# Splitting the mixer's weights ahead of time, in the first FFN, and keeping them in DRAM as halves

## The chip, the cores and the metric

The kernel runs on one core of a Trainium2 chip. The metric is the device time of one execution in microseconds (us). Engines are named as in the profile: PE is the tensor engine, DVE the vector engine, ACT the scalar engine, POOL is GpSimd, and SP is the engine whose queue issues the DMAs here.

## The reference

One step of an encoder layer on 1056 rows (1024 of a prompt, 32 of a running stream) of width 1024:

```python
x = x + 0.5 * swiglu(rmsnorm(x, g_ffn1), w1g, w1u, w1d)          # first FFN, 1024 -> 2816 -> 1024
mix, k, v, s = token_mixer(rmsnorm(x, g_mix), w_in, ...)         # the mixer
x = x + mix
x = x + 0.5 * swiglu(rmsnorm(x, g_ffn2), w2g, w2u, w2d)          # second FFN
return rmsnorm(x, g_final), k, v, s
# token_mixer: h @ w_in gives q, k, v of 8 stick-breaking heads (64 wide) and q, k, v, r of 4
# heads of gated linear attention (GLA); y = concat(norm(o_sb), norm(o_gla) * silu(r)) @ w_out
```

Everything is float32. The tensor engine multiplies operands that are rounded to a shorter form (`F32R`), so the kernel writes each operand as a sum of two halves, hi and lo, and makes three products: hi*hi, hi*lo, lo*hi.

## The kernel before

**The split.** `split_to` makes the halves: ACT copies the source to hi, which rounds it, and then DVE (or, with `pool=True`, POOL) subtracts hi from the source to get lo. `mm3` makes the three products. Activations lie with the feature on the partition: `S.x[d]` (8 tiles of 128x1056, float32) and `S.h[d]` (their halves, 128x2x1056).

**The stages.** First FFN: gate and up products, then down products; the mixer; the second FFN, built as the first. In the FFNs, gate and up weights are worked off in 20 steps (`gate_up`, ten pairs of a gate step and an up step, class `Step`). Each step makes the seven products of a Strassen-Winograd scheme in the order `ORDER = (1, 6, 7, 5, 2, 4, 3)`, 24 matmuls of 264 columns each. While a step's products run, the sums and splits of the next step's weights are made (`prep`, `split_w`; POOL makes the sums). After an up step, the hidden blocks B11, B22, B21 and four differences of them (T1, T3, T2, T4) are split and stored to DRAM by `keep`, from where the down stage reads them as parts. `keep` uses four of the x tiles in turn as its buffers; `S.x[4]` to `S.x[7]` hold the blocks.

**The mixer.** Each weight slab of 128x1024 is loaded by `load_split`: a DMA into a buffer of pool `raw` (two buffers, tile `wraw`, 512 KB), and then a split into a buffer of pool `wp` (two buffers, tile `whl`). The lo half comes from POOL in 24 projections (`proj`, from `w_in`) and in the four slabs `slab_a` of `w_out`; for the last four slabs (`slabs_b`, in a pool of their own, `slb`) it comes from DVE. A projection is 3 chunks of 352 columns by 8 feature tiles by 3 products, 72 matmuls (tile `pj`); an output group is 12 matmuls (tile `po`). The work on PE is interleaved: `run(items, fill)` spreads the fillers (projections, output groups) among the items (the blocks of an attention), in proportion to their costs. There are two GLA rounds and then four rounds of stick-breaking attention, one for each pair of heads. A block of scores is two sigmoids on ACT, a running product (the scan) and a product on DVE, transposes on PE, a split by ACT and DVE, and the value product on PE.

**The gates.** The four projections of r (`gate(0)` to `gate(3)`) multiply the GLA output. Two of the outputs lie in `S.x[6]`, `S.x[7]`, and two are parked in DRAM (`os`). The last round but one (pair 2) has `gate(1)` and then `gate(3)` as its last fillers; at the start of pair 3 the four gated outputs are split into `S.h[4]` to `S.h[7]`, chunk by chunk, and `ready(k)` splits the outputs of the first three pairs into `S.h[0]` to `S.h[2]` with POOL.

**What sets the order.** The code gives the work in program order; a scheduler then places each instruction in its engine's stream by its own estimate. At run time every engine, and SP's queue of DMAs too, works strictly in its order: a DMA whose wait is not over holds up all those behind it on SP.

## Time and profile before

| | |
|---|---|
| three runs | 2151.09 us median (2148.07 to 2152.23) |
| the profiled execution | 2149.15 us, of which 2147.4 us is the span of instructions |
| granted TensorE clock, mean | 0.988 |
| PE / DVE / ACT / POOL busy | 2069.2 / 1442.3 / 892.2 / 742.8 us |
| first FFN, gate and up steps | from about 86 us to about 500 us |
| first FFN, down | to 737 us |
| mixer | 737 us to about 1400 us |
| second FFN | from there to the end |

The profile is read by stage: which engine is never idle there, and what ends the idle time of PE where PE has some. A busy PE is not a PE at its peak, since matmuls overlap; the distance between the starts of two matmuls tells the pace. `PEclk` is the clock that was granted to PE, as a share of full speed.

### The profile page before, as it was taken

The page shows a single profiled execution, that of the slowest core. Times are in us where ns is not written, and L with a number is a line of the kernel's source. Part 1 is how long each engine was busy: PE and PEld are TensorE (multiplying, and loading weights), DVE is VectorE, ACT ScalarE, POOL GpSimd, SP SyncE. Part 2 cuts the span into 40 slices and gives each one's busy share as a digit, 9 for nine tenths or more (in the row PEclk, how much of TensorE's full clock was granted, in tenths as well). Part 3 has the DMA queues.
Part 4 walks back from the last instruction along what each step waited for, and adds up shares of the span by engine and source line. Part 5 has one row for each costly group of instructions (what it writes and reads, how often), then busy time and mean ns, then how long its engine had stood idle before and what let it go on. Part 6 is the DMA issues. An engine that isn't in the chain of part 4 may idle for free.

```text
span 2147.4 us, 38446 instructions
## 1 busy us (share of the span) xinstructions
PE 2069.2 (96%) x15636; PEld 1998.0 (93%) x15636; DVE 1442.3 (67%) x2142; ACT 892.2 (42%) x1586; POOL 742.8 (35%) x609
## 2 busy tenths in 40 slices
PE   7999999999999999999999988899999999999997
PEld 6899999999999978888888987899999999999997
DVE  6856756646786766286776687687567667467865
ACT  6533433432233443335555555454334333322333
POOL 0134334345872321122223312101343343458720
PEclk9999999999999999999999999999999999999999
DMA  5134434449823200102203141231344334498322
GB/s 174 50 120 152 161 121 154 168 139 379 303 94 117 87 32 30 38 31 67 77 23 100 36 124 69 78 123 51 120 159 156 127 143 168 139 376 300 106 65 82
DMA packets 106705, 270.49 MB, mean 126 GB/s; under 512 B 10432, under 2 KB 31200, under 8 KB 106528
## 3 DMA queue, kind: packets, MB, share of 16 engines
q1 hardware_dynamic: 106528, 268.03, 35.6%
q8 instruction: 123, 2.02, 0.4%
q14 instruction: 54, 0.44, 0.1%
HBM read 174.46 MB, written 86.77 MB: 122 GB/s over the span
## 4 chain that ended last, share of the span: by engine, by line
PE 77%; DVE 13%; ACT 3%; issue 3%; DMA 2%; POOL 1%; DVEq 0%; SPq 0%; ACTq 0%; POOLq 0%
PE acc_a L335 11%; PE acc_c L335 11%; PE acc_d L335 11%; PE acc_b L335 5%; PE acc L243 4%; PE pj L60 3%; PE pj L61 3%; PE pj L62 3%; PE pd_c L516 3%; PE pd_a L516 2%; PE pd_d L516 2%; DVE f L1206 2%; PE pd L60 2%; PE pd L62 2%; PE pd L61 2%
## 5 line engine op out<-in xcount | busy, mean ns | idle before, releaser
L335 PE MATMUL acc_a<-h,whl 128*128 128x264 f32 x1920 | 250.1, 286 | 1.8 <-DVE whl L55 1.8
L335 PE MATMUL acc_d<-part,S 128*128 128x264 f32 x1920 | 246.6, 284 | 0.0
L335 PEld LDWEIGHTS acc_a<-h,whl 128*128 128x128 f32 x1920 | 241.6, 190 | 2.1 <-DVE whl L55 2.1
L335 PEld LDWEIGHTS acc_d<-part,S 128*128 128x128 f32 x1920 | 238.7, 188 | 0.0
L60 PE MATMUL pj<-h,whl 128*128 128x352 f32 x576 | 203.9, 354 | 0.0
L61 PE MATMUL pj<-h,whl 128*128 128x352 f32 x576 | 191.1, 332 | 0.0
L62 PE MATMUL pj<-h,whl 128*128 128x352 f32 x576 | 190.8, 331 | 0.0
L51 ACT ACTIVATE S<-s 128x512 fp32r<-128x512 f32 x160 | 98.7, 627 | 183.6 <-PE acc_d L335 77.0
L51 ACT ACTIVATE x<-x 128x528 fp32r<-128x528 f32 x112 | 72.4, 647 | 180.8 <-DVE x L394 84.8
L319 POOL TENSOR_TENSOR s<-wraw,s 128x512 f32<-128x512 f32 x38 | 49.1, 1292 | 278.9 <-DVE S L55 278.9
L385 POOL TENSOR_TENSOR x<-tc,x 128x528 f32<-128x528 f32 x60 | 103.6, 1727 | 120.0 <-DVE tc L384 107.4
L53 POOL TENSOR_TENSOR whl<-wraw,whl 128x1024 fp32r<-128x1024 f32 x28 | 69.4, 2480 | 169.9 <-ACT whl L51 169.8
L55 DVE TENSOR_TENSOR x<-x 128x528 fp32r<-128x528 f32 x112 | 85.3, 761 | 63.1 <-ACT x L51 60.8
L335 PE MATMUL acc_b<-h,S 128*128 128x264 f32 x960 | 125.5, 286 | 1.5 <-ACT h L51 1.1
L335 PE MATMUL acc_c<-part,S 128*128 128x264 f32 x960 | 124.3, 284 | 0.3 <-DVE hid L255 0.3
L55 DVE TENSOR_TENSOR S<-s,S 128x512 fp32r<-128x512 f32 x160 | 122.0, 763 | 3.7 <-ACT S L51 2.5
L335 PE MATMUL acc_c<-h,A 128*128 128x264 f32 x960 | 124.2, 285 | 0.0
L335 PEld LDWEIGHTS acc_b<-h,S 128*128 128x128 f32 x960 | 121.2, 189 | 1.9 <-ACT h L51 1.3
L534 POOL TENSOR_TENSOR x<-x,u 128x528 f32<-128x528 f32 x64 | 103.5, 1624 | 49.5 <-DVE x L505 49.0
L335 PEld LDWEIGHTS acc_c<-part,S 128*128 128x128 f32 x960 | 120.0, 188 | 0.6 <-DVE hid L255 0.6
L335 PEld LDWEIGHTS acc_c<-h,A 128*128 128x128 f32 x960 | 120.4, 188 | 0.0
L306 POOL TENSOR_TENSOR s<-wraw 128x512 f32<-128x512 f32 x38 | 48.9, 1288 | 195.6 <-DVE S L55 195.6
(344 smaller groups left out, 5122.4 us busy)
## 6 DMA issues: line engine op xcount, KB each, us to landing
part_spill<-x SPq DMA_DIRECT2D x112, 528.0 KB, 2.8
h<-part_spill SPq DMA_DIRECT2D x64, 528.0 KB, 8.9
part<-part_spill SPq DMA_DIRECT2D x48, 528.0 KB, 9.6
wraw<-win SPq DMA_DIRECT2D x24, 512.0 KB, 3.4
wraw<-w1g SPq DMA_DIRECT2D x22, 512.0 KB, 3.7
wraw<-w1u SPq DMA_DIRECT2D x22, 512.0 KB, 3.4
wraw<-w1d SPq DMA_DIRECT2D x22, 512.0 KB, 3.8
wraw<-w2g SPq DMA_DIRECT2D x22, 512.0 KB, 3.5
```

The costliest lines, as they stand in the source:

```text
L51: nc.scalar.activation(hi, src, AF.Copy)
L53: nc.gpsimd.tensor_sub(lo, src, hi.bitcast(F32))
L55: nc.vector.tensor_sub(lo, src, hi.bitcast(F32))
L60: nc.tensor.matmul(out, w[:, 0, wsl], a[:, 0, asl], start=first, stop=False)
L61: nc.tensor.matmul(out, w[:, 0, wsl], a[:, 1, asl], start=False, stop=False)
L62: nc.tensor.matmul(out, w[:, 1, wsl], a[:, 0, asl], start=False, stop=last)
L243: nc.tensor.matmul(out, self.w[i](k, a), quarter(S, k, b, j), start=k == 0 and n == 0, stop=k == KT - 1 and n == 2)
L319: eng.tensor_sub(src, a12, self.s2)
L335: nc.tensor.matmul(t[:, s, :SW], w[:, a, ks], m(k, b, s), start=fresh and k == 0 and n == 0, stop=k == 3 and n == 2, skip_group_check=not ...
L385: nc.gpsimd.tensor_mul(two(hid), t, sg)
L516: nc.tensor.matmul(t[:, s, :SW], w[:, u, k * P : k * P + P], b[:, v, ss(s)], start=fresh and k == 0 and i == 0, stop=k == 1 and i == 2, sk ...
L534: nc.gpsimd.tensor_add(x[r][h], x[r][h], u)
```

## The change

`Splits` makes the halves of all mixer weights during the gate and up steps of the first FFN: in 64 chores, four in each of the first 16 steps (after products 1, 7, 2 and 3), it loads half a slab (256 KB) into `S.x[2]` or `S.x[3]`, splits it there (ACT and DVE), and stores both halves (512 KB) to a DRAM tensor of its own (`win2`, `wo2`). In the mixer, `load_halves` reads a whole slab of halves (1 MB) by one DMA, right into the buffer that PE reads; the pool `raw` is not used there. Since two x tiles are now taken, `keep` has two buffers in turn and not four, in both FFNs, and the differences T1, T3, T2, T4 are made and kept one by one after the first four products of the following gate step (`forms`), and not together at the end of the up step.

The last two gates run in turns, chunk by chunk (`g1[c] + g3[c]`), each followed by the split of that chunk's gated outputs (`gated(c)`), so that no splits are left for the start of pair 3. `ready(k)` becomes nine splits by chunk, on ACT and DVE.

```diff
-def load_split(S, src, hi_pool, tag, pool=False):
-    raw = S.raw.tile([P, 1024], F32, name="wraw", tag="wraw")
-    nc.sync.dma_start(raw, src)
-    w = hi_pool.tile([P, 2, 1024], F32R, name="whl", tag=tag)
-    split_to(S, w[:, 0], w[:, 1], raw, pool)
+def load_halves(S, src, pool, tag):
+    w = pool.tile([P, 2, 1024], F32R, name="whl", tag=tag)
+    S.nc.sync.dma_start(w.bitcast(F32), src)
     return w
+class Splits:
+    def load(self):
+        src, _, h = self.todo[self.n]
+        b = self.raw[self.n] = self.bufs[self.n % len(self.bufs)][:, :1024]
+        self.S.nc.sync.dma_start(b[:, 512:], src[:, h * 512 : h * 512 + 512])
+        self.n += 1
+    def split(self, n):
+        _, out, h = self.todo[n]
+        b = self.raw.pop(n)
+        t = b.bitcast(F32R).rearrange("p (a n) -> p a n", a=2)
+        split_to(self.S, t[:, 0], t[:, 1], b[:, 512:])
+        nc.sync.dma_start(out[:, :, h * 512 : h * 512 + 512], b.rearrange("p (a n) -> p a n", a=2))
+    def some(self):
+        if self.n == 0:
+            self.load()
+        if self.raw:
+            n = self.n - 1
+            if self.n < len(self.todo):
+                self.load()
+            self.split(n)
...
-        t = S.x[S.n_kept % 4].bitcast(F32R).rearrange("p (a n) -> p a n", a=2)
+        t = S.x[S.n_kept % 2].bitcast(F32R).rearrange("p (a n) -> p a n", a=2)
...
             steps[t].after(p)
+            if steps[t].gate is None and t:
+                steps[t - 1].forms(ORDER.index(p))
+            if t < N - 1 and p in (1, 7, 2, 3):
+                chore()
...
-                hold["w"] = load_split(S, src, S.wp, "w", True)
+                hold["w"] = load_halves(S, src, S.wp, "w")
...
-                fills = [gate(2), gate(0), gate(1) + gate(3)]
+                g1, g3 = gate(1), gate(3)
+                fills = [flat(gate(2)), flat(gate(0)), flat([g1[c] + g3[c] + [(0, lambda c=c: gated(c))] for c in range(NCH)])]
...
-                        def ready(k):
-                            split_to(S, S.h[k][:, 0], S.h[k][:, 1], S.x[k], True)
-                            nc.sync.dma_start(S.x[k], xs[k])
+                        def ready(k, c):
+                            split_to(S, S.h[k][:, 0, cs(c)], S.h[k][:, 1, cs(c)], S.x[k][:, cs(c)])
+                            if c == NCH - 1:
+                                nc.sync.dma_start(S.x[k], xs[k])
...
-                    slabs_b = [load_split(S, A["wo"][4 + j], slb, "slb") for j in range(4)]
+                    slabs_b = [load_halves(S, A["wo2"][4 + j], slb, "slb") for j in range(4)]
```

PE's order in both FFNs stays as it was; in the mixer it shifts in places. Three places matter for what follows. In the rows a name is out<-in, and a number after a name tells buffers apart.

First, DVE in the first FFN, around the turn from an up step to the next gate step. `x_76` is the whole of the eight x tiles; 128x528 subtractions of it by L55 are `keep`'s splits, those of L394 make T1 to T4, and L351 and L354 read the products 6 and 7 of the gate step. Before:

```order
L55 TENSOR_TENSOR S4_2701<-s3_2699,S4_2701 128x512
L394 TENSOR_TENSOR x_76<-x_76 128x528 x2
L55 TENSOR_TENSOR x_76<-x_76 128x528
L394 TENSOR_TENSOR x_76<-x_76 128x528
L55 TENSOR_TENSOR x_76<-x_76 128x528
L394 TENSOR_TENSOR x_76<-x_76 128x528
L55 TENSOR_TENSOR x_76<-x_76 128x528 x2
L351 TENSOR_TENSOR u2_2760<-s1_2733,acc_b_2735 128x528
```

Now (L428 makes T1 to T4, L85 is the split, and its 128x512 rows on `x_76` are the chores):

```order
L85 TENSOR_TENSOR S4_2324<-s3_2322,S4_2324 128x512
L428 TENSOR_TENSOR x_76<-x_76 128x528 x2
L85 TENSOR_TENSOR x_76<-x_76 128x528
L428 TENSOR_TENSOR x_76<-x_76 128x528 x2
L85 TENSOR_TENSOR x_76<-x_76 128x528
L381 TENSOR_TENSOR u2_2391<-s1_2356,acc_b_2366 128x528
L85 TENSOR_TENSOR S2_2401<-s2_2399,S2_2401 128x512
L85 TENSOR_TENSOR x_76<-x_76 128x512
L384 TENSOR_TENSOR u3_2429<-u2_2391,acc_c_2404 128x528
L85 TENSOR_TENSOR S3_2441<-s3_2439,S3_2441 128x512
L85 TENSOR_TENSOR x_76<-x_76 128x528
```

Two of the four keeps moved behind the reads of products 6 and 7, and chores stand between them.

Second, DVE at the end of pair 2. `h6`, `h7`, `h4`, `h5` are the gated outputs' halves, `rs`/`x` the gating, `ks` an operand of pair 3. Before, all twelve splits of gated outputs stand after the last scan of pair 2, eight of them behind `ks`:

```order
L1137 TENSOR_TENSOR ks_13389<-kf_12656,ks_13389 64x1056
L55 TENSOR_TENSOR wt_13250<-tr_13339,wt_13250 128x4x128
L55 TENSOR_TENSOR h6_90<-x_76,h6_90 128x352
L55 TENSOR_TENSOR h4_88<-h4_88 128x352
L55 TENSOR_TENSOR h5_89<-h5_89 128x352
L55 TENSOR_TENSOR h4_88<-h4_88 128x352
L55 TENSOR_TENSOR h5_89<-h5_89 128x352
L1178 TENSOR_TENSOR x_76<-avt_13375,av_13358 64x256
```

Now:

```order
L85 TENSOR_TENSOR wt_13440<-tr_13526,wt_13440 128x4x128
L85 TENSOR_TENSOR h0_84<-x_76,h0_84 128x352
L85 TENSOR_TENSOR h1_85<-x_76,h1_85 128x352
L85 TENSOR_TENSOR wt_13441<-tr_13543,wt_13441 128x4x128
L1175 TENSOR_TENSOR ks_13603<-kf_12849,ks_13603 64x1056
L85 TENSOR_TENSOR h6_90<-x_76,h6_90 128x352
L1216 TENSOR_TENSOR x_76<-avt_13579,av_13562 64x256
```

Only the last chunk's four are left there; the splits of `h0` and `h1` that POOL made now stand on DVE.

Third, SP at the end of the mixer: the loads of the output slabs. Before, the last two of `slab_a`, then `slabs_b` (from `wraw_14425` on), the reload of x tile 3, and the second FFN's first weights:

```order
L42 DMA wraw_14199<-wo 128x1024
L42 DMA wraw_14425<-wo 128x1024
L42 DMA wraw_14430<-wo 128x1024
L42 DMA wraw_14435<-wo 128x1024
L1581 DMA x_76<-x_spill 128x1056
L42 DMA wraw_14440<-wo 128x1024
L220 DMA wraw_14747<-w2g 128x1024
```

Now:

```order
L41 DMA whl_14303<-wo_split 128x2048
L41 DMA whl_14386<-wo_split 128x2048
L317 DMA wraw_15643<-w2g 128x1024
L41 DMA whl_14609<-wo_split 128x2048
L1623 DMA x_76<-x_spill 128x1056
L41 DMA whl_14611<-wo_split 128x2048
L41 DMA whl_14613<-wo_split 128x2048
L41 DMA whl_14615<-wo_split 128x2048
```

`slabs_b` are now the last four rows but for the reload of x tile 3 (L1623), which stands ahead of three of them, where it was ahead of one; and a weight load of the second FFN (`wraw_15643`), which takes a buffer that the second FFN's first slab leaves when it is split, stands ahead of all four.

More of the change, by code (lines that the diff above doesn't have):

```diff
@@ L826, in put @@
         return cb
-    return [proj(S, A["win"][16 + 2 * hp + h], put(h)) for h in range(2)]
+    return [proj(S, A["win2"][16 + 2 * hp + h], put(h)) for h in range(2)]
 def gla_items(S, A, G, hp, vs):
@@ L1450, in between @@
                     emit(parts(H))
[L1452 removed]
+            gate_up(S, H, op, steps, among, between, down.head, A["x"], Splits(S, A, (S.x[2], S.x[3])).some)
             nc.vector.tensor_copy(S.identb, consts[:, 0])
```

59 lines of the change are left out of this document (33 added, 26 removed).

## The prediction

> **What bounds the kernel now.** I read the chain of waits and the windows by stage first, then the waits inside the mixer, then its time line. The chain of waits by engine and by line first, then windows; their columns are length, busy time of PE, weight loads, DVE, ACT and POOL, granted clock, DMA share, GB/s:
>
> ```profile
> PE 77%; DVE 13%; ACT 3%; issue 3%; DMA 2%; POOL 1%; DVEq 0%; SPq 0%; ACTq 0%; POOLq 0%
> PE acc_a L335 11%; PE acc_c L335 11%; PE acc_d L335 11%; PE acc_b L335 5%; PE acc L243 4%; PE pj L60 3%; PE pj L61 3%; PE pj L62 3%; PE pd_c L516 3%; PE pd_a L516 2%; PE pd_d L516 2%; DVE f L1206 2%; PE pd L60 2%; PE pd L62 2%; PE pd L61 2%
> ...
> 86.00:500.00 414.00, 414.00 (x3375) 414.00 (x3376) 257.89 (x332) 152.21 (x239) 170.44 (x118) 0.99 0.42 154
> 500.00:520.00 20.00, 20.00 (x166) 20.00 (x165) 14.71 (x21) 5.64 (x10) 12.43 (x10) 1.00 1.01 378
> 730.00:1400.00 670.00, 630.86 (x4290) 570.38 (x4289) 457.81 (x721) 331.50 (x631) 159.20 (x159) 0.97 0.20 62
> 1400.00:1440.00 40.00, 40.00 (x327) 39.87 (x326) 36.27 (x97) 22.39 (x54) 0.00 (x0) 1.00 0.33 102
> 1484.00:1900.00 416.00, 416.00 (x3414) 416.00 (x3414) 253.28 (x328) 152.36 (x240) 166.68 (x117) 1.00 0.42 154
> ```
>
> The gate and up steps of both FFNs are bound by PE alone: it is never idle, the other engines are busy half the time, DMA moves 154 GB/s where 378 is reached at share 1.01. Work put there is free while those margins last; nothing can be won there. The mixer is the one long stage with idle PE: 670 - 630.9 = 39.1 us, and a clock of 0.97. So the change can win little more than 39 us and what the clock loses.
>
> **The change part by part. 1: chores in the first FFN (cost 0).** Groups of the page and of the lines view, and the time to landing of DMAs:
>
> ```profile
> L55 DVE TENSOR_TENSOR S<-s,S 128x512 fp32r<-128x512 f32 x160 | 122.0, 763 | 3.7 <-ACT S L51 2.5
> L51 ACT ACTIVATE S<-s 128x512 fp32r<-128x512 f32 x160 | 98.7, 627 | 183.6 <-PE acc_d L335 77.0
> L55 DVE TENSOR_TENSOR x<-x 128x528 fp32r<-128x528 f32 x112 | 85.3, 761 | 63.1 <-ACT x L51 60.8
> L51 ACT ACTIVATE x<-x 128x528 fp32r<-128x528 f32 x112 | 72.4, 647 | 180.8 <-DVE x L394 84.8 <-POOL x L385 81.6 <-DVE x L381 13.4
> L394 DVE TENSOR_TENSOR x<-x 128x528 f32<-128x528 f32 x64 | 62.2, 971 | 20.2 <-POOL x L385 19.7
> part_spill<-x SPq DMA_DIRECT2D x112, 528.0 KB, 2.8
> h<-part_spill SPq DMA_DIRECT2D x64, 528.0 KB, 8.9
> 99.99 2.94 PE acc_c L335 x24
> ```
>
> 64 chores add 64 x 0.763 = 48.8 us to DVE (306.7 of 414) and 64 x 0.627 = 40.1 us to ACT (192.3 of 414). Their DMAs move 64 x 768 KB = 50 MB in 16 steps of 7 x 2.94 = 20.6 us, 329 us: 153 GB/s more, 307 of 378. All fits. The tightest deadline on DVE is the read of a product before its accumulator is used again, three products (8.8 us) later; split weights are made about five products ahead of their use. Keeping in two buffers: a buffer comes round after two products, 5.9 us, and is held for 0.65 (ACT) + 0.76 (DVE) + the landing; with 2.8 us that is 4.2, plus 0.97 for the difference ahead of it. It fits as long as landings stay under about 3.5 to 4.5 us, and beyond that the wait is ACT's, with those margins behind it. I take 0; the ends are 0 and the first rival. The second FFN has the same ring without chores: 0.
>
> **2: splits taken out of the steady mixer (-12).**
>
> ```profile
> PE tr L1218 <- DVE w L1207: 4.8, 8, 1.2
> L51 ACT ACTIVATE whl<-wraw x32: 1038/1054/1097, 738.1 to 1390.5; 128x1024 fp32r<-128x1024 f32 x32
> L53 POOL TENSOR_TENSOR whl<-wraw,whl 128x1024 fp32r<-128x1024 f32 x28 | 69.4, 2480 | 169.9 <-ACT whl L51 169.8
> 1240.03 2.40 POOL L53 TENSOR_TENSOR whl<-wraw,whl 128x1024 fp32r<-128x1024 f32 x1 [0.72 <-ACT whl L51]
> 1240.57 2.94 DVE L1206 TENSOR_TENSOR_SCAN f<-f 128x512 f32<-128x512 f32 x1 [1.08 <-ACT f L1203]
> 1245.29 1.49 DVE L1206 TENSOR_TENSOR_SCAN f<-f 128x640 f32<-128x640 f32 x1
> 1244.39 0.55 PE L1218 MATMUL tr<-consts,w 128*128 128x128 f32 x3 [0.91 <-DVE w L1207]
> 1259.40 2.39 POOL L53 TENSOR_TENSOR whl<-wraw,whl 128x1024 fp32r<-128x1024 f32 x1
> 1259.93 2.25 DVE L1518 TENSOR_TENSOR oc<-oc,rs 128x352 f32<-128x352 f32 x1
> 1253.81 0.52 DVE L1518 TENSOR_TENSOR oc<-oc,rs 128x352 f32<-128x352 f32 x1
> ```
>
> About 32 x 1.05 = 34 us of ACT and 69 us of POOL go. Few matmuls wait for these splits directly; those that wait in the mixer name DVE first (the first row, of 1200 to 1430 us). What they do is slow DVE: beside POOL's 2.40 us at 1240 a scan of 512 columns took 2.94 us, and one of 640 took 1.49 without it; at 1259 a product took 2.25 us and the same one 0.52 elsewhere. Each time DVE lost about 1.7 us. What of it reaches PE differs: after the first, PE stood 0.91 us for the scan's successor; after the second it had projections to do. The mean, 0.45 us, by 27 splits that lie in this stretch gives 12 us. Ends: 0 (DVE is late, PE has fillers) and 27 x 0.91 = 25.
>
> **3: the start of pair 3 (-7).**
>
> ```profile
> 1272.53 5.11 POOL L53 TENSOR_TENSOR h<-x,h 128x1056 fp32r<-128x1056 f32 x2 [4.81 <-ACT h L51]
> 1275.40 3.35 DVE L1137 TENSOR_TENSOR ks<-kf,ks 64x1056 fp32r<-64x1056 f32 x1
> 1262.21 1.26 DVE L1136 TENSOR_TENSOR ks<-kf,ks 64x1056 fp32r<-64x1056 f32 x1
> 1279.53 1.76 PE L1231 MATMUL av<-wt,vs 128*128 128x256 f32 x7 [4.62 <-DVE wt L55]
> 1275.00:1280.00 5.00, 0.47 (x2) 0.47 (x3) 4.94 (x5) 1.40 (x4) 2.64 (x1) 0.94 0.03 7
> 1280.00:1285.00 5.00, 5.00 (x22) 5.00 (x22) 3.90 (x9) 3.06 (x7) 0.00 (x0) 0.50 0.81 285
> 1285.00:1290.00 5.00, 5.00 (x37) 4.86 (x37) 2.09 (x6) 1.62 (x5) 1.38 (x1) 0.88 0.42 139
> ```
>
> Two of the `ready` splits on POOL stretch DVE's `ks` from 1.26 to 3.35 us, a queue of splits stands around it, and PE waits 4.62 us; then the clock is 0.50 for 5 us and 0.88 for 5 more, which costs 2.5 + 0.6. Together 7.7 us. After the change POOL splits nothing there and DVE has eight fewer gated splits in that place. What may take its place is the first output slab, 1 MB into a buffer that the gates hold to their end; but other matmuls of pair 3 stand ahead of it on PE. I take 7; ends 0 and 9.
>
> **4: `ready` on DVE (+1).** Nine splits at the 0.52 us of the 352-column row above are 4.7 us of DVE, spread from pair 2's end into pair 3. By the share of part 2 (0.45 of 1.7) 1.2 us reach PE. Ends 0 and 4.7.
>
> **5: the last four output slabs (+6).** Rows of the chain (the last output group of pair 3), of SP, POOL, ACT and PE, and the landing of one load:
>
> ```profile
> 1376.57 0.17 PE po L62
> 1300.50 79.83 SPq L42 DMA_DIRECT2D wraw<-wo  x4
> 1383.60 0.33 SPq L42 DMA_DIRECT2D wraw<-wo  x1
> 1380.04 2.46 POOL L53 TENSOR_TENSOR h<-x,h 128x1056 fp32r<-128x1056 f32 x1 [5.67 <-ACT h L51]
> 1388.05 1.06 ACT L51 ACTIVATE whl<-wraw 128x1024 fp32r<-128x1024 f32 x1 [0.67 <-DMA wraw<-wo]
> 1389.16 0.39 PE L60 MATMUL po<-h,whl 128*128 128x264 f32 x1 [0.27 <-ACT whl L51]
> wraw<-wo SPq DMA_DIRECT2D x8, 512.0 KB, 3.4
> ```
>
> Before, three of the four came early into `raw` or were issued by 1380.3, and the fourth at 1383.60 let PE go on at 1389.16. Now three of them stand on SP behind the reload of x tile 3, which waits for POOL's last split, done at 1380.04 + 2.46 = 1382.5. 1 MB takes 3.4 us and another 512 KB at 378 GB/s, 1.4, so 4.8. With the reload (528 KB, 1.4 us) ahead, the three land at about 1389, 1391.8 and 1394.6: the last is 5.4 us later than PE's start now. The first of the four waits behind the second FFN's weight load and so for that split (ACT 1.05, DVE 1.2 or more, from the last use of its buffer, one group of 12 x 0.16 us before the last one's end at 1376.7), and lands near 1383, while PE has only the norm's nine transposes after 1376.7, to about 1378. Such an idle stretch of some 5 us is followed by a slow clock, as at 1280, which DVE's and SP's lateness partly hides: I add 1. Sum +6; ends 0 (the loads go out earlier than I think) and 10 (all of the waits and the clock).
>
> [...]
>
> **6: the boundary to the mixer (0).** The first projection's buffer comes free before the end of the down stage and 4.8 us fit in; the second's comes free at its end and lands, by the same 4.8 us, about when the first's 24 matmuls and a statistic are done. Ends 0 and +2. The four splits of the last slabs on ACT and DVE go too; that stage is PE's (40.00 of 40.00), so 0.
>
> **Sum.** -12 - 7 + 1 + 6 = -12. The profiled execution took 2149.15 us (span 2147.4), 1.9 under the median of 2151.09. 2149.15 - 12 = 2137.2, and against the median 2139.
>
> **The rivals.**
>
> *The splits were hidden.* PE's order in the mixer is fixed, DVE is late there for the scans' own sake (the chain of waits gives the scan alone 2%), and a shorter DVE only waits more for ACT. For it: the second sample of part 2, where PE lost nothing. Against it: 39 us of idle PE whose waits name DVE. Then part 2 is 0 to -4 and the sum -7 + 1 + 6 - 2 = -2: 2149, no change.
>
> *The ring of two and the DMAs bind the first FFN (slower).* ACT works in order; a keep whose buffer has not landed stops it. In a pair of steps (41.2 us) ACT is busy 152.2/414 x 41.2 + 8 x 0.627 = 20.2 us, and seven keeps each wait for 2.4 + landing - 5.9. PE is caught when this passes the 21 us left: at a landing of 6.5 us. At 7 us it costs 7 x 3.5 - 21 = 3.5 us a pair, over eight pairs 28 us: 2139 + 28 = 2167. For it: landings of 8.9 us where the DMA share is 1.01. Against it: the share here would be about 0.8, and the bytes are spread.
>
> *The late slabs cost more.* If the four loads come as late as in part 5's upper end and the first output slab also comes late, parts 3 and 5 cancel: -12 - 3 + 1 + 10 = -4, 2147.
>
> **How the numbers follow.** My forecast (2130 to 2146) has 0.62, the hidden splits 0.16, the slower case 0.11, the late slabs 0.11. A change of 0.2%, 4.3 us, is about what a measurement of this kernel can tell from none. Faster than 2146.8: the forecast's 0.62, half of the late slabs, a little of the hidden splits and as much from a better mixer, 0.73. Within 0.2%: 0.15. Slower: 0.12. The range takes the forecast down to the lower end of part 2 (25 for 12 would give 2126) and up to the hidden splits: 2127 to 2153; the slower rival is left out.
>
> **What would show it.** Right: PE still 414 of 414 in the first FFN's gate and up steps, with DVE near 307 and DMA share near 0.8; mixer scans of 512 columns at 1.2 us throughout and no 2.9; no 4.6 us gap at the start of pair 3, and a clock near 1.00 there; a gap of some 5 us, then shorter ones, where `po` goes over to the `wo_split` slabs. Wrong: landings of `part_spill` over 6 us with PE idle behind DVE or ACT in the first FFN; the mixer's idle PE still near 39 us with the splits gone (part 2); PE waiting for DMA at `pj` or `po`.

## The result, and the profile after

The changed kernel takes 2177.84 us (median of 4 runs, 2175.96 to 2180.02) against 2151.02 for the kernel before: 1.012 times as long, 95% interval 1.0104 to 1.0136. The forecast was 2139. Medians here and below leave out one execution each of e9 and e11, of 5072 and 6964 us. The page of the changed kernel, in this order: span; shares of the chain of waits; the two rows that hold the chores (with keep's splits, of nearly the same shape); DMAs with size and median time to landing:

```profile
span 2173.8 us, 38757 instructions
...
PE 66%; DVE 13%; DMA 8%; issue 6%; ACT 4%; POOL 3%; SPq 0%; DVEq 0%; ACTq 0%; POOLq 0%
...
L81 ACT ACTIVATE x<-x 128x528 fp32r<-128x528 f32 (+1 forms) x176 | 111.0, 638 | 291.4 <-POOL x L415 94.8
L85 DVE TENSOR_TENSOR x<-x 128x528 fp32r<-128x528 f32 (+1 forms) x176 | 143.7, 823 | 118.7 <-ACT x L81 118.3
...
part_spill<-x SPq DMA_DIRECT2D x112, 528.0 KB, 2.9
...
win_split<-x SPq DMA_DIRECT2D x48, 512.0 KB, 3.7
...
x<-win SPq DMA_DIRECT2D x48, 256.0 KB, 4.0
...
wraw<-w1u SPq DMA_DIRECT2D x22, 512.0 KB, 5.7
```

Before, the chain of waits was PE for 77% and DMA for 2%; now PE has 66% and DMA 8%. ACT's and DVE's rows have mean times of 638 and 823 ns, where 627 and 763 were forecast for a chore; what is new is what stands behind the second bar: DVE idle 118.7 us, nearly all of it for ACT's hi.

Where the time went shows by stage, from the first matmul of each to the first of the next, in both traces. Gate and up steps of the first FFN: 417.9 before, **450.5** after. Down and plain products: 171 both, 71 both. First projection to the 4200th matmul behind it, where the last output slabs are at work: 657.3 and **652.6**. Gate and up of the second FFN: 409.7 both. So the loss, +32.6, lies in one stage, the mixer brings about -5, and the second FFN, which has the moved differences and the ring of two but no chores, costs nothing. The first step of the stage lasts 27 to 29 us and differs by some 1 us from trace to trace, so differences of 1 us in this stage mean nothing.

In that stage, first the window (length, busy time of PE, weight loads, DVE, ACT and POOL, granted clock, DMA share, GB/s), then the waits of PE, DVE and ACT from 90 to 520 us (total, times, longest):

```profile
90.00:527.00 437.00, 413.78 (x3309) 408.88 (x3309) 305.94 (x387) 179.79 (x302) 164.87 (x116) 0.99 0.72 255
```

```profile
PE acc_c L365 <- DVE u L384: 19.0, 14, 3.7
...
DVE x L85 <- ACT x L81: 78.8, 50, 3.8
...
ACT x L81 <- POOL x L415: 53.9, 16, 4.1
ACT x L81 <- issue: 51.8, 13, 4.6
ACT x L81 <- DMA x<-win: 34.6, 23, 3.8
...
ACT x L81 <- DMA part_spill<-x: 19.9, 11, 2.9
```

DVE is busy 306 us, the forecast's 307; the DMA share is 0.72; and PE, which waited for nothing here before, waits for `u L384`, DVE's read of product 7, without which product 4 cannot go into the same accumulator. The waits are not all of the loss: over the whole stage PE is idle 24.2 us longer (27.8 against 3.6), and its busy time for the same matmuls is 8.4 us longer (422.7 against 414.3). Three of the steps have a granted clock of 0.93, and PE is busy 22.3 us in each instead of 20.5; one of them:

```profile
190.51:216.45 25.94, 22.28 (x171) 22.07 (x169) 14.70 (x19) 11.51 (x20) 7.44 (x6) 0.93 0.70 250
```

The chain of waits there (start, length, what), and some of DVE's instructions, with the idle time before each and what ended it:

```profile
188.02 5.34 DMA win_split<-x
193.38 6.00 DMA x<-win
199.48 0.64 ACT x L81
200.15 0.70 DVE x L85
200.87 3.27 DMA win_split<-x
204.15 2.69 DMA x<-win
206.95 0.64 ACT x L81
207.64 0.57 issue
208.22 0.70 DVE u L384
```

```profile
201.18 0.70 DVE L381 TENSOR_TENSOR u<-s,acc_b 128x528 f32<-128x528 f32 x1 [0.34 <-ACT s L378]
205.59 0.69 DVE L85 TENSOR_TENSOR x<-x 128x512 fp32r<-128x512 f32 x1 [3.10 <-ACT x L81]
207.61 0.69 DVE L85 TENSOR_TENSOR x<-x 128x512 fp32r<-128x512 f32 x1 [1.33 <-ACT x L81]
208.22 0.70 DVE L384 TENSOR_TENSOR u<-u,acc_c 128x528 f32<-128x528 f32 x1
```

Read the chain downwards: a chore's store lands, which frees its buffer; only then does the load of the chore after next go out into it; ACT's hi waits for that load, DVE's lo for the hi, the next store for the lo. One turn of a buffer here took 200.87 - 188.02 = 12.9 us, and with the medians of the page 4.0 + 0.64 + 0.70 + 3.7 = 9.0. Four chores in a step of 20.5 us on two buffers allow 10.3. DVE's read of product 7 (`u L384`) stands behind two such lo in DVE's order, which waited 4.4 us, and PE behind the read, 3.7 us. In this trace what the read needs was there well before: product 7's last matmul ends at 199.47 and `u L381` at 201.88, but `u L384` starts at 208.22, 0.61 us after the second lo (207.61, 0.69 us long).

### The profile page after: what moved, and what is told of

Its sections match the earlier page's. It is cut to its first block, busy times and chain, and to the rows that moved or that the text cites. A ratio compares the mean times of both kernels' runs of the same rounds, so it can differ in the third digit from the quotient of the medians.

```text
span 2173.8 us, 38757 instructions
## 1 busy us (share of the span) xinstructions
PE 2083.5 (96%) x15636; PEld 2011.0 (93%) x15636; DVE 1468.3 (68%) x2211; ACT 890.6 (41%) x1624; POOL 661.3 (30%) x578
## 4 chain that ended last, share of the span: by engine, by line
PE 66%; DVE 13%; DMA 8%; issue 6%; ACT 4%; POOL 3%; SPq 0%; DVEq 0%; ACTq 0%; POOLq 0%
PE acc_a L365 7%; PE acc_d L365 7%; PE acc_c L365 6%; PE acc L273 4%; PE pj L90 3%; PE acc_b L365 3%; PE pj L91 3%; PE pj L92 3%; PE pd_c L554 3%; PE pd_d L554 3%; PE pd_a L554 3%; PE pd L90 2%; PE pd L92 2%; PE pd L91 2%; DMA x<-win 2%
## 5 line engine op out<-in xcount | busy, mean ns | idle before, releaser
L81 ACT ACTIVATE x<-x 128x528 fp32r<-128x528 f32 (+1 forms) x176 | 111.0, 638 | 291.4 <-POOL x L415 94.8
L85 DVE TENSOR_TENSOR x<-x 128x528 fp32r<-128x528 f32 (+1 forms) x176 | 143.7, 823 | 118.7 <-ACT x L81 118.3
L365 PE MATMUL acc_c<-h,A 128*128 128x264 f32 x960 | 130.1, 293 | 19.0 <-DVE u L384 19.0
L85 DVE TENSOR_TENSOR S<-s,S 128x512 fp32r<-128x512 f32 x160 | 124.3, 778 | 2.2 <-ACT S L81 1.5
L90 PEld LDWEIGHTS pj<-h,whl 128*128 128x128 f32 x576 | 111.9, 194 | 6.0 <-issue 1.5
L91 PEld LDWEIGHTS pj<-h,whl 128*128 128x128 f32 x576 | 112.1, 195 | 2.5 <-issue 0.7
```

What stands on the lines that cost most here:

```text
L81: nc.scalar.activation(hi, src, AF.Copy)
L85: nc.vector.tensor_sub(lo, src, hi.bitcast(F32))
L90: nc.tensor.matmul(out, w[:, 0, wsl], a[:, 0, asl], start=first, stop=False)
L91: nc.tensor.matmul(out, w[:, 0, wsl], a[:, 1, asl], start=False, stop=False)
L365: nc.tensor.matmul(t[:, s, :SW], w[:, a, ks], m(k, b, s), start=fresh and k == 0 and n == 0, stop=k == 3 and n == 2, skip_group_check=not ...
```

## The experiments

The theory after the first reading (called loop, waiting or turn-round theory in the expectations) was that the chores wait for their own transfers, since two buffers turn round too slowly, and that what stands behind them in ACT's and DVE's order is late. Against it stood: the work itself on ACT and DVE (compute, or load theory); 50 MB more in the DMA engines (traffic); keep's ring of two and the moved differences (ring). The chores are called splits in the expectations. "Gate/up" is the stage above. In the runs that read one slab throughout, `A["win2"]` and `A["wo2"]` are lists of that one slab.

**No chores (e1).**

```diff
-self.todo = [... for i in range(A[src].shape[0]) for h in range(2)]   # 64 chores
+self.todo = [(A["win"][i], A["win3"][i], h) for i in range(1) for h in range(2)]
```

> The changed kernel with one weight slab split in the first FFN instead of 32; every projection and output group of the mixer reads that one split slab, so the mixer's arithmetic is done on the wrong weights and only its time is meant. Keep's ring of two and the moved differences of the parts stay. Loop theory (two buffers, each held over load, split and store, serve the splits too slowly): the first gate/up falls from 450.5 us back to 418, the whole to 2178 - 32.7 = 2145 us. Compute theory (ACT and DVE time of the splits) and traffic theory (48 MB more in the DMA engines) say the same here. Ring theory (two tiles for kept parts instead of four, and the moved differences): gate/up stays near 450, the whole near 2178. The mixer up to the last gates is as before the change by all of them, since between the first projection and the 3200th matmul after it both traces are within 3.4 us.

Measured: 2141.76 us, 0.9952 of before (0.9940 to 0.9965), gate/up 418.0. The ring theory falls: with ring and moved differences left in, the stage is what it was. All of the loss comes with the chores, and without them the change would be a gain of 10 us.

**Chores without transfers (e2), without stores (e3), without loads (e4).**

```diff
 def load(self):
-    self.S.nc.sync.dma_start(b[:, 512:], src[...])          # left out from chore 2 on: e2, e4
 def split(self, n):
-    nc.sync.dma_start(out[...], b.rearrange(...))           # left out from chore 2 on: e2, e3
```

> As the run with one slab, but all 64 splits stay on ACT and DVE, on data that lies in the two buffers; loads and stores only for the first two (the mixer reads one slab throughout, so the output is not the reference's). Loop theory and traffic theory: no transfer is waited for, gate/up 418 to 421 us, whole 2145 to 2149. Compute theory: gate/up 450, whole 2178; anything between is the share of ACT's 64 x 0.64 and DVE's 64 x 0.70 us that shows.

> All 64 splits with their loads of 256 KB, but stores only for the first two (the mixer reads one slab throughout, so the output is not the reference's). Loop theory: a buffer is free as soon as it is split, the round trip of two splits falls from about 4.0 + 0.64 + 0.70 + 3.7 = 9.0 us (which with its scatter meets the 10.3 us that two splits have) to 5.3, gate/up 418 to 422, whole 2145 to 2150. Traffic theory: a third of the bytes stays, so about a third of 32.7 us: gate/up 429, whole 2156. Compute theory: 2178.

> All 64 splits with their stores of 512 KB, on data that lies in the buffers; loads only for the first two (the mixer reads one slab throughout, so the output is not the reference's). Loop theory: the round trip of two splits is 0.64 + 0.70 + 3.7 = 5.0 us and no load stands in SP's order behind a store's landing; but ACT now waits for the store of two splits before: gate/up 418 to 424, whole 2145 to 2152. Traffic theory: two thirds of the bytes stay: gate/up 440, whole 2167. Compute theory: 2178.

Measured: 2156.77 (1.0025, 1.0014 to 1.0037), gate/up 436.8; 2171.17 (1.0089, 1.0076 to 1.0103), 449.4; 2169.69 (1.0077, 1.0059 to 1.0096), 446.5. No one theory fits all three, and the reason is in the order: with a transfer gone the chores stand closer together in the order that the scheduler makes, 11 to 17 in a step (e2), 7 or 8 (e3), 5 to 7 (e4) instead of 3 to 5 on DVE. The loss lies in those steps alone; behind them every step has 20.5 us. One step of e2 (windows):

```profile
124.50:153.00 28.50, 22.64 (x169) 21.86 (x169) 28.50 (x35) 16.07 (x28) 11.81 (x8) 0.94 0.46 166
```

DVE is busy 28.50 of 28.50 us: drawn together, the chores are too much for it. That is another loss than the changed kernel's, whose DVE is busy 70% of the time. Since the order changed with the transfers, the three runs can't tell what the transfers cost.

**The same, kept in place (e7, e9, e10).** `keep_in_program_order` ties each hi and lo behind the instruction ahead of it in the code on its engine, and a step has 3 to 5 chores again.

```diff
-    split_to(self.S, t[:, 0], t[:, 1], b[:, 512:])
+    split_to(self.S, t[:, 0], t[:, 1], b[:, 512:], pin=True)   # hi and lo kept behind what the code has ahead of them
```

> As the run with splits but no transfers (the mixer reads one slab throughout, so the output is not the reference's), now with each split kept behind the instruction ahead of it in the code, on ACT and on DVE. Without that the scheduler had drawn the splits together, up to 17 in a step; so held, a step has 3 to 5, as in the changed kernel. Waiting theory: gate/up 418 to 421 us against 436.8 with the splits drawn together, whole 2142 to 2146. Load theory: gate/up 435 to 450, whole 2160 to 2175.

> The changed kernel, complete, with each split kept behind the instruction ahead of it in the code on ACT and on DVE: 4 in every step instead of 5 and 3 in turns. Placement theory (most of the 32.7 us comes from splits that the scheduler set close together or ahead of a product's read): gate/up 420 to 430, whole 2147 to 2158. Waiting theory (the splits wait for their transfers wherever they stand, since two buffers turn round in about 9 of 10.3 us) and traffic theory: gate/up 442 to 452, whole 2170 to 2180.

> The kept-in-place splits (3 to 5 in a step) with their loads of 256 KB, without their stores (the mixer reads one slab throughout, so the output is not the reference's). Without transfers this was 419.1 us in gate/up. Waiting theory: the load is issued one split, 4 to 6 us, ahead and lands in 4.3, so that it is late by little: 421 to 428, whole 2144 to 2152; the larger part of the 32.7 us belongs to the store and what it holds up. Traffic theory: a third of 31 us: 429, whole 2153. Should the load alone bring 440 or more, SP's order is what holds it (it is issued behind other transfers that wait for DVE).

In the fourth (e11), every chore still computes, loads and stores, but what is loaded, what is split and what is stored are three separate pieces of memory (`keep` below is `keep_in_program_order`, and the code is shortened):

```diff
-    sync.dma_start(b[:, 512:], src[...])                    # into the buffer that is split
+    keep(sync.dma_start(slot, src[...]))                    # into the other tile
-    sync.dma_start(out[...], b.rearrange(...))              # the halves just made
+    keep(sync.dma_start(out[...], S.h[0][:, :, :512]))      # an operand that lies still
```

> All 64 splits on ACT and DVE on one tile, all 64 loads and stores at the same places of SP's order, but into and from other memory, so that no split waits for a transfer and no transfer for a split (what is stored is not the split, and the mixer reads one slab throughout: the output is not the reference's). Waiting theory: 418 to 422 us in gate/up, whole 2140 to 2146. Traffic theory (48 MB more make the other transfers late): 440 to 450, whole 2163 to 2175.

Measured, in this order: computing alone 2139.42 (0.9932, 0.9914 to 0.9951), gate/up **419.1**; complete 2181.49 (1.0122, 1.0098 to 1.0146), **457.2**; with loads 2143.83 (0.9962, 0.9945 to 0.9979), **420.9**; apart 2141.41 (0.9953, 0.9937 to 0.9968), **416.9**. One window of each, in the same order:

```profile
104.00:450.00 346.00, 345.56 (x2829) 344.98 (x2828) 272.85 (x345) 160.31 (x269) 141.73 (x92) 1.00 0.41 147
```

```profile
104.00:450.00 346.00, 322.08 (x2540) 318.01 (x2539) 231.96 (x310) 147.55 (x246) 129.33 (x83) 0.98 0.74 260
```

```profile
104.00:450.00 346.00, 344.12 (x2807) 342.47 (x2807) 268.99 (x343) 159.52 (x268) 137.83 (x92) 1.00 0.56 192
```

```profile
104.00:450.00 346.00, 346.00 (x2839) 346.00 (x2838) 275.69 (x346) 162.05 (x270) 145.54 (x94) 1.00 0.82 287
```

The fourth row decides. DVE does more in these 346 us than in the other three, the DMA engines move the most of all (287 GB/s, share 0.82), and PE is never idle. So neither compute nor traffic costs anything here; the link between the chores and their own transfers does. One thing besides the link differs: in e11 the issues of the chores' DMAs are kept in place too, so that SP has another order than in the complete run, and what that order alone is worth was not tested. With loads and no stores (e10) the stage is 1.8 us longer than with computing alone (2.8 without the first step): a load whose buffer is free once it is split is nearly in time. That the chores stand close together falls as the cause: complete and evenly placed, they cost more than in the changed kernel.

**The same space used otherwise, complete kernels.** e5 and e12 take one tile for two raw half slabs and the other for one pair of halves, so that no load waits for a store; e8 halves the chores (128 of 256 columns, four raw places, two split ones); e16 has five raw places and three for the hi.

```diff
-b = self.raw[self.n] = self.bufs[self.n % len(self.bufs)][:, :1024]
+b = self.raw[self.n] = self.bufs[0][:, self.n % 2 * 528 :][:, :512]   # e5, e12 (kept in place)
+b = self.raw[self.n] = self.bufs[0][:, self.n % 4 * 264 :][:, :256]   # e8
+b = self.raw[self.n] = self.at(self.n % 5)                            # e16 (kept in place), lo made in it; hi in self.at(5 + n % 3)
```

> The changed kernel, complete, with the two buffers of the splits used otherwise: one tile holds two raw half-slabs, loaded two splits ahead, the other the two halves of one split until its store has landed. No load waits for a store any more, and a load has some 10 us until it is read. Waiting theory (the splits wait for transfers, and DVE's read of product 7 stands behind them): the 34.6 us that ACT waits for loads from win go; what stays is ACT's wait for the store of the split before, issued 5 us earlier against a landing of 3.7: gate/up 450.5 to 420-428, whole 2147 to 2156. Load theory (ACT and above all DVE have no room for four more instructions in a step of 20.5 us): gate/up stays over 440, whole over 2168.

> The changed kernel, complete, with one tile for two raw half-slabs loaded two splits ahead and one for the split halves, and the splits kept in their places, none beside another. Unpinned this was 449.9 us in gate/up with ACT waiting 70 us for the stores of splits just before. If the bunching made those waits: a store of 3.4 us has 4 to 6 us, gate/up 421 to 428, whole 2145 to 2155. If a store is late by itself, since it is issued behind DVE's second half and SP's other transfers: 440 to 450, whole 2165 to 2175.

> The changed kernel, complete, with quarter slabs: 128 splits of 256 columns, one behind each product, in the same two tiles: four raw quarters (each loaded four splits, 11.7 us, ahead) and two split ones (a store has 5.9 us until its place is used again). Waiting theory: neither transfer is waited for except where a landing is over 5.9 us: gate/up 419 to 424, whole 2144 to 2151. Load theory: twice as many instructions with their fixed part, gate/up 450 or more, whole 2178 or more.

> The changed kernel, complete, with 128 splits of 256 columns kept in their places, one behind each product, and the two tiles cut in eight places: five for raw quarters, in which the lower half then stands until it is stored, three for the upper half. A raw place has 14.6 us for load 3.5, split 0.8 and store 3.5, an upper one 8.8 us for split and store. Turn-round theory: gate/up 419 to 428, whole 2146 to 2156. Theory 'every wait for a store costs', or SP's order with 384 small transfers in place of 128: 445 or more, whole 2170 or more.

Measured: e5 2173.68 (1.0093, 1.0079 to 1.0107), gate/up 449.9; e12 2176.49 (1.0108, 1.0092 to 1.0125), 451.9; e8 2189.85 (1.0167, 1.0153 to 1.0181), 466.2; e16 2168.06 (1.0069, 1.0055 to 1.0083), 444.1. My expectations by the waiting and turn-round theory, from 419 to 428, were wrong: I had counted when a store is issued and not that its place is taken until it lands. ACT's waits in e12 (90 to 490 us):

```profile
ACT x L82 <- DMA win_split<-x: 58.1, 25, 3.8
```

The wait for the load has turned into one for the store: one place for halves is held 0.64 + 0.70 + 3.5 us (the landing there), about 4.8, of the 5.1 that a chore has. e8's two places of half the size at twice the pace are held 0.41 + 0.61 + 3.5 = 4.5 of 5.9 us, and ACT waits 64.2 us for its stores. e16 is the best of the four and still slow, and it speaks against the turn-round as the whole account: a raw place is held 3.5 + 0.41 + 0.59 + 3.1 = 7.6 of its 14.6 us, half the time, and yet ACT waits 32.2 us for the loads and the stage loses 26 us. The rival expectation, SP's order (445 or more), came nearer. In e16 a load is issued only two chores, 5.9 us, ahead, and SP waits 60.8 us for ACT and 21.2 for DVE with stores of halves, which stand ahead of later loads; that this makes the loads late was not tested, and what is left in e16 is open.

**Wider spacing, same buffers.** Only the 24 slabs of `win`, 48 chores; the slabs of `wo` are split in the mixer with POOL, as before (the last four too, where it was DVE). In e13 the chores are kept in place, three in each step; e18 has the same chores left to the scheduler, which sets four in a step on DVE.

```diff
-for src, out in (("win", "win2"), ("wo", "wo2"))
+for src, out in (("win", "win2"),)
-if t < N - 1 and p in (1, 7, 2, 3):
+if t < N - 1 and p in (7, 2, 3):
-load_halves(S, A["wo2"][j], S.wp, "w")
+load_split(S, A["wo"][j], S.wp, "w", True)      # and the four last slabs likewise
```

> The changed kernel, complete, but only the 24 slabs of win are split in the first FFN, 48 splits, behind products 7, 2 and 3 (three in every step, kept in their places); the eight slabs of wo are split in the mixer by GpSimd as before. A buffer's round trip of 9 us or a little more then has 13.7 us instead of 10.3. Turn-round theory: gate/up 418 to 424, whole 2138 to 2148, faster than before. Theory 'every wait for a store costs': 48/64 of 32.7, gate/up 442, whole 2163. At the last output slabs the raw slabs are 512 KB as before, so the 6 us there should be gone if the slabs' size made them, and stay if x3's reload did.

> The 48 splits of win, complete, written behind products 7, 2 and 3 but not kept there: the scheduler sets them four and five in a step over twelve steps, 4.1 to 5.1 us apart, where they were 6.8 apart. Same number, same bytes, same buffers. Turn-round theory: twelve steps lose as the changed kernel's sixteen did, 2.0 us each: gate/up 417.3 + 24 = 441, whole 2169. Theory 'it is the number and the bytes': gate/up 417 to 422, whole 2145 to 2150.

Measured: e13 **2145.32** (0.9963, 0.9950 to 0.9977), gate/up **417.3**; e18 **2178.89** (1.0118, 1.0102 to 1.0134), **448.7**. The same chores, bytes and buffers; ACT's wait for the loads in the one and in the other, and one row of the windows of each:

```profile
ACT x L92 <- DMA x<-win: 26.7, 15, 4.2
```

```profile
104.00:450.00 346.00, 345.79 (x2836) 345.58 (x2835) 259.12 (x330) 153.69 (x255) 145.14 (x93) 1.00 0.72 252
```

```profile
ACT x L91 <- DMA x<-win: 67.0, 25, 5.6
```

```profile
104.00:450.00 346.00, 324.66 (x2579) 321.10 (x2578) 232.77 (x304) 139.66 (x234) 126.76 (x85) 0.98 0.66 237
```

With three chores in a step, 13.7 us for two, the stage loses nothing; with four, 10.3 us for two, it loses 30.8. (e17 below has e13's chores once more: 418.6.) So the same number, bytes and buffers cost nothing or all of it, and e13 also beats the kernel before.

How the spacing helps shows on DVE, ahead of its read of product 7 in a gate step. In the kernel before (86 to 495 us) DVE waited there for PE, 4.5 us a step for product 6 and 1.5 for product 7:

```profile
DVE u L351 <- PE acc_b L335: 49.6, 11, 4.5
...
DVE u L354 <- PE acc_c L335: 16.3, 11, 1.5
```

In the same place the chores of e13 make DVE wait 0.5 to 4.8 us a step; those of e9, kept in place as well, 2.6 to 7.1, those of the changed kernel 2.9 to 7.8, those of e18 6.5 to 9.7. The longest in e13, with the reads of products 6 (`acc_b`) and 7 (`acc_c`) behind it:

```profile
193.62 0.69 DVE L93 TENSOR_TENSOR x<-x 128x512 fp32r<-128x512 f32 x1 [4.85 <-ACT x L92]
194.23 0.70 DVE L395 TENSOR_TENSOR u<-s,acc_b 128x528 f32<-128x528 f32 x1
195.45 0.70 DVE L398 TENSOR_TENSOR u<-u,acc_c 128x528 f32<-128x528 f32 x1
```

So e13's chores still wait for their loads, but within time in which DVE had nothing to do before; with four chores in a step the waits go beyond it and PE waits too. Two limits remain. e13 also leaves out the chore behind product 1, one of the two that stand in this place in e9, so spacing and place changed together. And e16's chores make DVE wait only 0.4 to 2.2 us there, so its 26 us came another way. What is shown is that chores which wait for their own transfers, with reads behind them that free PE's accumulators, cost the 32.6 us; how that divides between turn-round, place and SP's order is open.

**The mixer.** All kernels have the same number of matmuls in it, so they can be laid side by side by that number: us from the first projection to the n-th matmul behind it, before, and the difference of the others (one trace each).

| n | before | after | e1 no chores | e14 halves only | e13 win only | e6 turns only | e15 x3 late |
|---|---|---|---|---|---|---|---|
| 2000 | 300.9 | +1.7 | +1.3 | +3.6 | 0.0 | +3.8 | 0.0 |
| 3200 | 484.6 | -0.1 | -0.5 | +0.1 | -1.6 | +6.4 | -3.7 |
| 4000 | 626.2 | -10.8 | -12.2 | -9.6 | -6.8 | +3.2 | -13.4 |
| 4200 | 657.3 | -4.7 | -6.2 | -3.5 | -1.5 | +3.3 | -9.2 |

How far such differences carry can be read from the record: 13 of the kernels (after, e1 to e5, e7 to e12, e16) have the very same order on PE, DVE and ACT in the mixer. At the 3200th matmul they lie between -8.8 (e16, 475.8 us at a granted clock of 0.99) and +2.2 (e10, 486.9 us at 0.96). From there to the 4000th they win 9.6 to 11.9, and to the 4200th they give back 4.4 to 8.1. So the row of 3200 tells nothing between versions, e15's -3.7 and e6's +6.4 included.

e6 is the kernel before with the gates in turns and `ready` by chunks alone; e14 is e1 with both of these as before, the gates one after the other and `ready` on POOL. The line of the gates in e6:

```diff
-fills = [gate(2), gate(0), gate(1) + gate(3)]
+fills = [flat(gate(2)), flat(gate(0)), flat([g1[c] + g3[c] + [(0, lambda c=c: gated(c))] for c in range(NCH)])]
```

> The kernel before with one part of the change alone: the last two gates in turns by chunks, and the three tiles before the last output slabs split in chunks on DVE. No halves in DRAM, no splits in the first FFN, keep and its differences as before, GpSimd splits the mixer's weights as before. Theory 'all of the mixer's gain lies in the turns' (steady mixer not bound by GpSimd's splits): first FFN as before, pair 3 starts 8 to 11 us earlier, and what the last output slabs give back (6.1 us in the changed kernel, whose slabs are 1 MB) falls or stays: 2151 - 10.8 + (0 to 6) = 2140 to 2146. Theory 'the split weights bring some of it': 2146 to 2151, since 4 us or more of the changed mixer's gain would be missing.

> The mixer with split slabs (one slab read throughout, so the output is not the reference's; one slab split in the first FFN) and the last two gates in the order of before: first one gate, then the other, and the split of the gated tiles at the start of pair 3. Theory 'turns and halves each bring their part' (turns alone lost 6.3 us over the steady mixer and won 3 at pair 3): the mixer up to matmul 3200 as in the run with one slab, -0.5 against before, and 3 us of that run's 12.2 at pair 3 missing: whole 2141.8 + 3 = 2145. Theory 'the halves bring all': 2142. Theory 'only both together bring it': 2150 or more.

Measured: e6 2152.11 (1.0000, 0.9991 to 1.0009); e14 2142.55 (0.9948, 0.9934 to 0.9961). Between the 3200th and the 4000th matmul, the start of pair 3, the halves alone win 9.7, the turns alone 3.2, both 10.7 (11.7 in e1). The turns are worth little here: the splits of POOL that went are most of it. Both my theories for e6 were too hopeful: its steady mixer is 6.4 longer, of which 5.7 is PE's busy time at a granted clock of 0.97 (0.98 before) and 0.7 idle, within what the 13 kernels above differ by with one order.

From 4000 to 4200 every version with halves gives back 4 to 8, and e13, whose output slabs are 512 KB as before, 5.3: the larger transfer is not needed for it. e15 is e1 with the reload of x3 behind the four slabs, e17 is e13 with the same:

```diff
-nc.sync.dma_start(S.x[3], xs[3])                            # ahead of outs()
 slabs_b = [load_halves(S, A["wo2"][4 + j], slb, "slb") for j in range(4)]
+tc.keep_in_program_order(nc.sync.dma_start(S.x[3], xs[3]))
```

> The run with one slab, with the reload of x3 moved behind the four last slabs in SP's order (the mixer reads one slab throughout, so the output is not the reference's). Theory of the prediction (the reload waits for GpSimd's split of x3 and holds the slabs behind it): the 6.1 us at the last output slabs go, whole 2141.8 - 6 = 2136. Theory 'size' (1 MB in 5.6 us instead of 512 KB): they stay, whole 2141 to 2142; a slab that waits for its place until PE is done with it would show the same.

> The run with 48 splits (win alone), complete, with the reload of x3 issued behind the loads of the four last slabs. If the reload, which waits for GpSimd's split of x3, held the raw slabs: the 3.6 us wait ahead of the 4116th matmul and most of the 6.1 us at the last slabs go, whole 2145.3 - 4 to 6 = 2139 to 2141. If the raw slabs wait for their own split (GpSimd's second halves, 3 us each, in a row behind its split of x3): no change, 2144 to 2146.

Measured: e15 2139.40 (0.9935, 0.9922 to 0.9947); e17 2143.66 (0.9954, 0.9940 to 0.9967), which can't be told from e13. The stretch gives back 4.2 in e15 instead of e1's 6.0, which is no more than the kernels with one order differ by. In the chain of waits of e1, then of e15:

```profile
1369.15 2.41 POOL h L83
...
1371.58 0.32 SPq L1623
...
1371.95 5.80 DMA whl<-win_split
```

```profile
1363.05 0.88 PE tr L784 x8
1363.93 5.45 DMA whl<-win_split
1369.43 0.59 PE po L90
```

In e1 slabs stand behind POOL's split of x3 and the reload, as the prediction had it; with that gone, the first slab's own 5.45 us are left, which the chain lets begin when PE's transposes are done. PE's waits for these slabs say what the reload was worth: 5.3 us in two waits in e1, 4.5 in one in e15, so 0.8. The 4.5 for the first slab stands in both.

## Why the prediction was wrong

**Part 1 (cost 0) failed, and with it the forecast.** It counted the chores' busy time against the engines' and their bytes against 378 GB/s, and both came true (DVE 306 us; share 0.72, and 0.82 without loss when nothing is linked). The step that failed is "All fits", a cost put at 0 (it was +32.6 us): for keep's ring it had set up the sum of what a buffer is held, and for the chores' own two buffers, with load, hi, lo and store, it had not. That sum, from rows it quoted or had, is 0.65 + 0.76 + 2.8 for a store and as much for a load, 7.0 us at the landings of before and 9.0 at those after, against 10.3, with 1.3 left for scatter, where the turn shown above took 12.9. Nor did it ask who stands behind a chore that waits: on ACT hi and keep, on DVE the reads that free PE's accumulators. That these waits are the cost is shown by e11 against e9; that the sum of holding alone decides is not (e16). Also the deadline was too long: product 7 is at the third place, product 4 at the sixth, so between them lie two products, 5.9 us, not 8.8.

**The slower rival** had the place, the first FFN, and with 2167 came nearest of all to the time, with a chance of 0.11; that was luck, for its mechanism was not the one. Its landing of 6.5 us for kept parts was 2.9, and the ring of two costs nothing (418.0 in e1, 409.7 in the second FFN).

**Part 2 (-12) was 0 in the profiled execution, and -6.8 in one at the clock of before.** The premise held, in part: after the change the eight 512-column scans take 1.21 to 1.23 us, none 2.94; but before it only one of the eight had been slow, the one beside a split of POOL (2.40 us), and the seven without such a split beside them took 1.21 to 1.22. Why that one is slow was not tested further. But the 485 us of steady mixer stay 485 (windows of before, then of after, then of e8, whose mixer has the same order as after):

```profile
737.00:1222.00 485.00, 463.76 (x3204) 415.66 (x3203) 321.34 (x515) 237.57 (x442) 118.95 (x116) 0.98 0.17 50
```

```profile
769.00:1254.00 485.00, 470.36 (x3206) 423.77 (x3204) 303.19 (x512) 217.12 (x418) 62.51 (x94) 0.96 0.23 74
```

```profile
784.20:1262.00 477.80, 462.42 (x3203) 415.94 (x3201) 303.16 (x512) 216.67 (x418) 62.33 (x94) 0.98 0.23 75
```

DVE is freed of 18.1 us, PE's idle time falls from 21.2 to 14.6, and PE's busy time for as many matmuls rises by the same 6.6, with a granted clock of 0.96 instead of 0.98. In e8 the clock is 0.98 as before and the gain is there: 477.8 us instead of 484.6. So the 0 is partly chance of one trace. In the 13 kernels with this order PE is idle 13.9 to 17.7 us here, 3.5 to 7.3 less than before. The step that failed is the mean of 0.45 us a split: 12 us were forecast and the idle time gave 3.5 to 7.3, while PE's busy time here ranges over 12 us with the clock (459.3 to 471.3 in the 13). Whether the changed mixer draws a lower clock on the whole is open, since the kernel before has one trace. "The splits were hidden" was the rival nearest to the profiled execution.

**Part 3 (-7) named the right wait and was too small,** -10.7: the 4.62 us wait is gone, and the splits of the early output slabs went too (the win-only kernel, which keeps them, wins 5.2). Part 2 had counted those four splits at 0.45 us each. Of the mechanism only a part is shown. e14 keeps the `ready` splits on POOL and the gated splits at this place, its `ks` is stretched as well, and yet PE waits little there (DVE of before, just behind the `ks` of 3.35 us at 1275.40, then DVE and PE of e14):

```profile
1278.78 0.69 DVE L55 TENSOR_TENSOR wt<-tr,wt 128x512 fp32r<-128x512 f32 x1
```

```profile
1270.42 0.68 DVE L85 TENSOR_TENSOR wt<-tr,wt 128x512 fp32r<-128x512 f32 x1
1271.13 2.79 DVE L1175 TENSOR_TENSOR ks<-kf,ks 64x1056 fp32r<-64x1056 f32 x1
1273.97 0.33 PE L1237 MATMUL z<-ks,qh 128*128 128x128 f32 x1 [1.26 <-DVE ks L1175]
```

In the kernel before, the split of `wt` for which PE waited stood behind the stretched `ks`; in e14, as in the changed kernel, it stands ahead of it. **Part 5 (+6) measured +6.1, and the total is right by luck.** The forecast was 5.4 us for the last slab, behind the reload, and 1 for the clock. PE waited once, for the first slab; the three behind the reload landed while PE was at work. Over these 200 matmuls PE is idle 2.7 us more than before (5.9 against 3.2), and its busy time at a clock of 0.86 instead of 1.00 is 3.4 longer (PE's wait, then two windows of after):

```profile
PE po L90 <- DMA whl<-wo_split: 4.6, 1, 4.6
```

```profile
1400.00:1406.00 6.00, 0.64 (x5) 0.32 (x3) 1.73 (x4) 1.08 (x1) 2.41 (x1) 0.86 0.69 262
1406.00:1411.00 5.00, 4.82 (x21) 4.51 (x21) 0.14 (x1) 0.00 (x0) 0.00 (x0) 0.50 0.94 338
```

**Part 6 (0)** was right: at the 200th matmul the two traces differ by 0.1 us. `ready` on DVE (part 4) lies inside part 3's stretch and was not measured alone. Together: 0 - 12 - 7 + 1 + 6 = -12 was forecast; in the two traces +32.6 in the first FFN, -4.7 in the mixer and -1.5 in the rest make the spans' +26.4 (2173.8 against 2147.4), and the medians differ by 26.8.

## What to carry to other kernels

Before calling work free because its engines and the DMA bandwidth have room, write down how long each buffer of it is held, from the issue of its load to the landing of its store, and divide by the buffers: if that is near the spacing (9.0 of 10.3 us here), the work may wait as it did here, and what stands behind it in its engine's order with it (here DVE's read of product 7, behind two lo that waited 4.4 us), so look also at that. A sum that fits is not yet a promise: e16 held its places half of the time and still waited. Fewer chores further apart in the same two buffers (0.9963 of before) did what four kernels with the space cut otherwise did not. An experiment that takes a transfer away from a scheduled kernel must hold the rest of the order in place, or it measures another order. And before a few us of one stage are read from one trace against another, look how far traces with the same order differ there.

## What the runs showed that I had not expected

Slower transfers need not cost anything: in the run with compute and traffic apart `w1u`'s slabs took 6.9 us to land instead of the 3.4 of before and PE was never idle. And the same instructions in the same order on PE, DVE and ACT took between 475.8 and 486.9 us for the steady mixer in 13 kernels, with granted clocks from 0.99 to 0.96. Why the clock differs there was not tested.
